# A two-layer decoder trunk: the down projection's seven-product scheme in two chunks of three groups instead of three of two, its sums read from PSUM by VectorE, and the SWA layer's norm factor and vector applied in one instruction

## The chip, the cores and the metric

One core of one Trainium2 chip. The metric is the device time of one execution in microseconds (us). Engines are named as the profile names them: PE (TensorE matmul), PEld (its weight loads), DVE (VectorE), ACT (ScalarE), POOL (GpSimd), SP (SyncE). A name such as L942 is line 942 of the kernel before.

## The reference, cut to what matters

512 tokens of width 1024 pass through two layers, a gated linear attention layer and a sliding-window attention (SWA) layer, each followed by a dense MLP of width 4096. Every sub-layer is wrapped in two norms:

```python
def rms_norm(x, w):
    y = x * lax.rsqrt(jnp.mean(x * x, axis=-1, keepdims=True) + NORM_EPS)
    return y * w

def sq_relu_mlp(h, w_up, w_down):
    return jnp.square(jax.nn.relu(h @ w_up)) @ w_down

for i in range(2):
    x = x + rms_norm(mixer(rms_norm(x, ln_mix_pre[i])), ln_mix_post[i])
    x = x + rms_norm(sq_relu_mlp(rms_norm(x, ln_mlp_pre[i]), w_up[i], w_down[i]), ln_mlp_post[i])
```

All is float32. The kernel multiplies in float32r with each operand split into a high part (a cast, on ACT) and a low part (source minus high, on DVE); a product takes three matmuls: high by high, high by low, low by high.

## The kernel before

The change touches two places: the MLP's down projection (`down`, run once in each of the two layers) and the norm ahead of the SWA layer (`prenorm`, run for four token tiles at the end of the first layer's down projection).

**Down projection.** The hidden activations (4096 wide) form 16 pairs of 256 rows, in eight groups g of two pairs; a group has four blocks a11, a12, a21, a22 (pair p by token half q). The first six groups (`SEVEN = 6`) are multiplied in the manner of Strassen: seven products of combined blocks instead of eight. They are taken in chunks of two groups, three chunks in a layer, each a call of `seven`. A call has seven phases, in the order 1, 2, 5, 3, 6, 7, 4. A phase does for each group of the chunk:

- `parts`: splits the group's weights v[g][p] (128x1024) into high and low, one ACT cast and one DVE subtraction through the helper lines L85 and L86, into two of the ten buffers of the pool "w";
- then starts the transfer that makes v[g][p] the next phase's combination: an accumulating DMA on POOL's queue (L947, `add`) that adds another block of weights from DRAM, or once a plain load on SP's queue (L951);
- `unit`: splits the activation block (128x512 in all) the same way into a slot of the pool "s" (25 slots);
- and then the matmuls: for token tile t = 0, all groups; for t = 1, all groups; six matmuls of 512 columns to each (L910 to L912). So a phase of two groups has 24.

After phase 2, four DVE instructions to each group (L955 to L958) combine the blocks in place and into `r5`.

Products 1, 5, 3 and 6 use the two PSUM banks of the tag "mm" in turn and are taken out by `collect`. Product 3 goes on adding in the banks of product 5; product 6 starts afresh in the same two banks. So phase 3 waits until `collect(5)` has read a bank, and phase 6 until `collect(3)` has. Products 2, 7 and 4 stay in PSUM (tags tp, ob, sc) over all chunks. `collect` does this: in the first chunk, two ACT copies into `sums[m]` (L942); in the later ones, two ACT copies into a slot `part` (L942) and one accumulating DMA on POOL's queue that adds it to `sums[m]` in SBUF (L944); for product 6 of the last chunk two DVE additions that read PSUM (L938).

Then DVE joins sums and banks (L972 to L976, and L980 and L982 for the banks B and E, which go on as the accumulators of the first output half), and groups 6 and 7 are added by plain products. In group 6 each weight pair (n, p) is loaded, split and multiplied with the four token tiles in the order t = 0 to 3; the first two tiles add to B (tag tp), the other two to E (tag sc).

**Norm ahead of the SWA layer.** For token tile t, `prenorm` squares x on ACT, multiplies x by the norm's vector on DVE into `xw` (L231), computes the factor r by five small POOL instructions, scales `xw` by r on ACT (L237), transposes it on PE (L240) and splits the result. The scaling is put by hand behind a count of products on PE (`later(4 * t + SCALE, ...)`, ordered by `tick`), and so are the transposes.

**Order.** The order of instructions on each engine is fixed when the program is built: earlier lines have priority, an instruction that by the builder's own costs isn't ready lets later ones pass, and buffers of a pool are given out as they come free. On the chip each engine then runs its list in order, so an instruction that waits holds back everything behind it on its engine.

Of the kernel before, what the change touches and what calls it, by code (L numbers as in the profile page):

```python
# [8 lines left out]
F32 = mybir.dt.float32  # L9
F32R = mybir.dt.float32r  # L10
U32 = mybir.dt.uint32
AF = mybir.ActivationFunctionType
ALU = mybir.AluOpType

P = 128
D = 1024
T = 512
NT = T // P
# [10 lines left out]
SEVEN = 6  # L29
# [6 lines left out]
ADD, SCALE, TURN, TURN_UP = 7, 11, 9, 7  # L36
# [4 lines left out]
def trunk(ctx: ExitStack, tc: tile.TileContext, x, vecs, g_qk, g_vg, g_lr, g_up, g_out,  # L41
          s_qkv, s_sinks, s_out, m_up, m_down, consts, out):
    nc = tc.nc
    act, dve, pe, pool = nc.scalar, nc.vector, nc.tensor, nc.gpsimd

    const = ctx.enter_context(tc.tile_pool(name="const", bufs=1))
    rawp = ctx.enter_context(tc.tile_pool(name="rawp", bufs=4))
# [11 lines left out]
    def name(s):  # L59
        nm[0] += 1  # L60
        return f"{s}_{nm[0]}"

    def slot(shape, dt=F32, n="s"):
        return sp.tile(shape, dt, tag="s", name=name(n))
# [102 lines left out]
    def later(when, insts):  # L167

        if ticks[0] is not None:
            plan.setdefault(when, []).extend(insts)  # L170
# [44 lines left out]
    def prenorm(t, wpre, hT):  # L215
        xt = x_t[t]
        xw = slot([P, D], n=f"xw{t}")
        if isinstance(hT, Blocks):
            for q in range(2):
                part = slice(q * 512, (q + 1) * 512)  # L220
                dve.tensor_mul(xw[:, part], xt[:, part], wpre[:, part])
                tb = tbank([P, 4, P])
                for k in range(4):
                    later(4 * t + TURN_UP, [pe.transpose(tb[:, k, :], xw[:, q * 512 + k * P:q * 512 + (k + 1) * P], ident)])
                hT.put(t, q, tb)
            return
        ss, v0 = small(2), small(1)
        for i in range(2):
            part = slice(i * 512, (i + 1) * 512)
            act.activation(junk, xt[:, part], AF.Square, accum_out=ss[:, i:i + 1])  # L230
            dve.tensor_mul(xw[:, part], xt[:, part], wpre[:, part])  # L231
        pool.tensor_scalar(v0, ss[:, 0:1], 1.0 / D, EPS, ALU.mult, ALU.add)
        r = rsqrt(ss[:, 1:2], 1.0 / D, base=v0)
        cols = slice(t * P, (t + 1) * P)
        for q in range(2):
            part = slice(q * 512, (q + 1) * 512)
            later(4 * t + SCALE, [act.activation(xw[:, part], xw[:, part], AF.Copy, scale=r)])  # L237
            tb = tbank([P, 4, P])
            for k in range(4):
                later(4 * t + TURN, [pe.transpose(tb[:, k, :], xw[:, q * 512 + k * P:q * 512 + (k + 1) * P], ident)])  # L240
            for kk in range(2):
                h, l = hT[2 * q + kk]
                split(h[:, :, cols], l[:, :, cols], tb[:, 2 * kk:2 * kk + 2, :])
# [643 lines left out]
    def down(layer, blk, post, done):  # L887
# [26 lines left out]
        sums = {m: slot([P, 2, 512], n=f"sum{m}") for m in (1, 5, 3, 6)}  # L914
        B, C, E = [tbank() for _ in range(2)], [bank(tag="ob") for _ in range(2)], [sbank() for _ in range(2)]

        def seven(gs, first, last):
            v, r5 = {}, {}
            for g in gs:
                v[g] = [rawp.tile([P, 1024], F32, tag="raw", name=name("raw")) for _ in range(2)]  # L920
                for p in range(2):
                    nc.sync.dma_start(v[g][p], source(g, p, 0))

            def phase(m, p, act_blk, acc, start, stop, after=None, cont=False):
                w, u = {}, {}
                for g in gs:
                    w[g] = parts(v[g][p])
                    if after:
                        after(g)
                    u[g] = unit(act_blk(g))  # L930
                for t in range(2):
                    for g in gs:
                        product(acc[t], u[g], w[g], t, start and g == gs[0], stop and g == gs[-1], cont)

            def collect(m, acc, direct=False):
                if direct:
                    for t in range(2):
                        dve.tensor_add(sums[m][:, t], sums[m][:, t], acc[t])  # L938
                    return
                to = sums[m] if first else slot([P, 2, 512], n=f"part{m}")  # L940
                for t in range(2):
                    act.copy(to[:, t], acc[t])  # L942
                if not first:
                    pool.dma_start(sums[m], to, accum_op=ALU.add)  # L944

            def add(p, q, n):
                return lambda g: pool.dma_start(v[g][p], source(g, q, n), accum_op=ALU.add)  # L947
            A = [bank() for _ in range(2)]
            phase(1, 0, lambda g: blk(g, 0, 0), A, True, True, add(0, 0, 1))
            collect(1, A)  # L950
            phase(2, 1, lambda g: blk(g, 1, 0), B, first, last, lambda g: nc.sync.dma_start(v[g][1], source(g, 1, 1)))  # L951
            for g in gs:
                a11, a12, a21, a22 = blk(g, 0, 0), blk(g, 1, 0), blk(g, 0, 1), blk(g, 1, 1)
                x = r5[g] = slot([P, 2, 256], n=f"r5{g}")
                dve.tensor_sub(x, a22, a21)  # L955
                dve.tensor_sub(a21, a11, a21)
                dve.scalar_tensor_tensor(out=a11, in0=x, scalar=-1.0, in1=a11, op0=ALU.mult, op1=ALU.subtract)
                dve.scalar_tensor_tensor(out=a12, in0=a11, scalar=-1.0, in1=a12, op0=ALU.mult, op1=ALU.subtract)  # L958
            A = [bank() for _ in range(2)]
            phase(5, 0, lambda g: r5[g], A, True, True, add(0, 1, 1))  # L960
            collect(5, A)
            phase(3, 1, lambda g: blk(g, 1, 0), A, False, True, add(1, 0, 1), True)
            collect(3, A)
            A = [bank() for _ in range(2)]
            phase(6, 0, lambda g: blk(g, 0, 0), A, True, True, add(0, 1, 0))
            collect(6, A, last)
            phase(7, 1, lambda g: blk(g, 0, 1), C, first, last)
            phase(4, 0, lambda g: blk(g, 1, 1), E, first, last)

        for c in range(0, SEVEN, 2):  # L970
            seven((c, c + 1), c == 0, c + 2 == SEVEN)
        dve.tensor_add(sums[6], sums[1], sums[6])  # L972
        dve.tensor_add(sums[3], sums[3], sums[6])
        for t in range(2):
# [3 lines left out]
        acc = [B + E, N]  # L978
# [12 lines left out]
        G = NF // 4  # L991
        for g in range(SEVEN, G):
            u, w = {}, {}
            for n in range(2):
                for p in range(2):
                    w[p, n] = load(g, p, n)
                    if n == 0:
                        for q in range(2):
                            u[p, q] = unit(blk(g, p, q))
                    if g < G - 1:  # L1000
                        for t in range(NT):
                            product(acc[n][t], u[p, t // 2], w[p, n], t % 2, False, False, True)
        ticks[0] = 0
        for t in range(NT):
            for n in range(2):
# [14 lines left out]
    first, raws, xws, rs, tbs, last = [], {}, {}, {}, {}, {}  # L1020
# [20 lines left out]
    for step in START.split():  # L1041
# [21 lines left out]
        if what == "q" and n == 0:  # L1063
# [3 lines left out]
            v = small(1)  # L1067
# [126 lines left out]
```

## Time and profile before

| | |
|---|---|
| median of 3 runs | 1087.16 us (1084.81 to 1090.80) |
| the profiled execution | 1085.77 us, of which span 1084.0 us |
| mean granted TensorE clock | 0.988 of full speed |
| busy: PE / DVE / ACT / POOL | 1047.5 / 772.3 / 679.5 / 179.3 us |
| first layer's down projection | about 400 to 572 us |
| second layer's down projection | about 904 to 1076 us |

A row of a timeline gives start, duration, engine, line, operation, and in square brackets the idle time ahead of the instruction and what ended it. Matmuls overlap in the pipeline: their durations are longer than the distance between their starts, and the distance is what counts. A row of the lines' view has busy time and mean duration, then idle time ahead and its releasers.

### The profile page before, as it was taken

Reading aid. Unit: us, or ns where it says so; the run is one execution under the profiler, and the core shown is the slowest. Engines: PE = TensorE matmul, PEld = TensorE weight load, DVE = VectorE, ACT = ScalarE, POOL = GpSimd, SP = SyncE. Lnnn points to the kernel's source line nnn. Section 1 sums busy time; section 2 is a strip of 40 time slices with the busy share of each in tenths; the row PEclk is TensorE's granted clock in tenths of the full one; section 3 lists DMA queues with packets and bytes.
Section 4 is the critical chain, followed back from the end, with each engine's and each line's share of the span. In section 5 each row is a group of like instructions: output and inputs, shape, how many; then the busy total and the mean of one; then the engine's idle time right before and its main releaser. Section 6 shows DMA issues by size and latency. Waiting matters only on the chain. (4 is left out here: it accounts for less than half of the span.)

```text
span 1084.0 us, 16766 instructions
## 1 busy us (share of the span) xinstructions
PE 1047.5 (97%) x6236; PEld 920.0 (85%) x6236; DVE 772.3 (71%) x1281; ACT 679.5 (63%) x1374; POOL 179.3 (17%) x345
## 2 busy tenths in 40 slices
PE   8999999999999999999998999999999999899997
PEld 5888888899999997877787899889999998677775
DVE  5666538588776867758746789779877777676764
ACT  7774436377676786556445688647766777665632
POOL 2001110256000011212025001027300001121202
PEclk9999999999999999999998999999999999999998
DMA  7323122232233267898714542012333336889922
GB/s 274 136 63 113 59 78 80 76 98 79 80 116 115 81 166 184 173 229 190 210 53 136 163 111 79 25 54 79 118 97 98 104 109 148 200 181 231 214 79 78
DMA packets 39220, 134.35 MB, mean 124 GB/s; under 512 B 4705, under 2 KB 4833, under 8 KB 39138
## 3 DMA queue, kind: packets, MB, share of 16 engines
q1 hardware_dynamic: 30210, 100.76, 29.1%
q0 software_dynamic: 8928, 32.51, 16.1%
q8 instruction: 49, 0.80, 0.3%
q14 instruction: 33, 0.27, 0.1%
HBM read 119.62 MB, written 2.10 MB: 112 GB/s over the span
## 5 line engine op out<-in xcount | busy, mean ns | idle before, releaser
L86 DVE TENSOR_TENSOR w<-raw,w 128x1024 fp32r<-128x1024 f32 x184 | 208.6, 1141 | 129.1 <-ACT w L85 127.2
L85 ACT CAST w<-raw 128x1024 fp32r<-128x1024 f32 x184 | 180.3, 982 | 129.6 <-DMA raw<-in_m_down_dram 53.4
L947 POOL DMA_DIRECT2D raw<-in_m_down_dram x48 | 42.3, 881 | 401.1 <-DVE a L855 261.2
L910 PE MATMUL mm<-w,u 128*128 128x512 f32 x224 | 90.6, 404 | 9.5 <-ACT part L942 5.3
L836 PE MATMUL A<-Sh,w 128*128 128x256 f32 x336 | 95.5, 284 | 0.0
L838 PE MATMUL A<-Sh,w 128*128 128x256 f32 x336 | 95.0, 283 | 0.0
L837 PE MATMUL A<-Sl,w 128*128 128x256 f32 x336 | 95.0, 283 | 0.0
L912 PE MATMUL mm<-w,u 128*128 128x512 f32 x224 | 89.6, 400 | 1.5 <-DVE u L86 0.9
L911 PE MATMUL mm<-w,u 128*128 128x512 f32 x224 | 88.8, 397 | 0.0
L85 ACT CAST wh<-raw 128x512 fp32r<-128x512 f32 x92 | 54.2, 621 | 30.8 <-PE ob L157 12.5
L86 DVE TENSOR_TENSOR wl<-raw,wh 128x512 fp32r<-128x512 f32 x92 | 60.3, 684 | 17.4 <-ACT wh L85 15.4
L836 PEld LDWEIGHTS A<-Sh,w 128*128 128x128 f32 x336 | 64.3, 191 | 1.2 <-ACT a L848 1.2
L837 PEld LDWEIGHTS A<-Sl,w 128*128 128x128 f32 x336 | 64.4, 192 | 0.0
L838 PEld LDWEIGHTS A<-Sh,w 128*128 128x128 f32 x336 | 64.4, 192 | 0.0
L910 PEld LDWEIGHTS mm<-w,u 128*128 128x128 f32 x224 | 43.0, 192 | 21.9 <-ACT part L942 6.6
L86 DVE TENSOR_TENSOR u<-a,u 128x512 fp32r<-128x512 f32 x88 | 57.0, 684 | 4.7 <-ACT u L85 4.7
L912 PEld LDWEIGHTS mm<-w,u 128*128 128x128 f32 x224 | 43.0, 192 | 13.5 <-DVE u L86 4.5
L911 PEld LDWEIGHTS mm<-w,u 128*128 128x128 f32 x224 | 43.2, 193 | 8.7
L85 ACT CAST u<-a 128x512 fp32r<-128x512 f32 x88 | 50.0, 621 | 0.0
L786 ACT ACTIVATE a<-a 128x256 f32<-128x256 f32 (+1 forms) x96 | 45.9, 491 | 1.3
L85 ACT CAST w<-tt 128x1024 fp32r<-128x1024 f32 x28 | 29.4, 1050 | 13.6 <-PE C L837 7.1
L86 DVE TENSOR_TENSOR w<-tt,w 128x1024 fp32r<-128x1024 f32 x28 | 34.2, 1222 | 2.3 <-ACT w L85 2.2
(387 smaller groups left out, 3306.3 us busy)
## 6 DMA issues: line engine op xcount, KB each, us to landing
raw<-in_m_up_dram SPq DMA_DIRECT2D x64, 512.0 KB, 3.6
raw<-in_m_down_dram SPq DMA_DIRECT2D x52, 512.0 KB, 5.8
raw<-in_m_down_dram POOLq DMA_DIRECT2D x48, 512.0 KB, 7.3
raw<-in_g_vg_dram SPq DMA_DIRECT2D x16, 512.0 KB, 4.1
sum<-part POOLq DMA_DIRECT2D x14, 512.0 KB, 8.9
raw<-in_s_qkv_dram SPq DMA_DIRECT2D x10, 512.0 KB, 3.6
raw<-in_g_qk_dram SPq DMA_DIRECT2D x8, 512.0 KB, 3.6
raw<-in_g_out_dram SPq DMA_DIRECT2D x8, 512.0 KB, 3.6
```

Source lines behind the costliest of these rows:

```text
L85: act.copy(h, src)
L86: dve.tensor_sub(l, src, f(h))
L786: act.activation(v, v, AF.Square)
L836: pe.matmul(acc, lhsT=wh[:, kc], rhs=h[:, k], start=first, stop=False, skip_group_check=not fresh)
L837: pe.matmul(acc, lhsT=wh[:, kc], rhs=l[:, k], start=False, stop=False, skip_group_check=not fresh)
L838: pe.matmul(acc, lhsT=wl[:, kc], rhs=h[:, k], start=False, stop=last, skip_group_check=not fresh)
L910: pe.matmul(acc, lhsT=ah[:, j, tc_], rhs=wh[:, wc], start=first and j == 0, stop=False, **kw)
L911: pe.matmul(acc, lhsT=ah[:, j, tc_], rhs=wl[:, wc], start=False, stop=False, **kw)
L912: newest[0] = pe.matmul(acc, lhsT=al[:, j, tc_], rhs=wh[:, wc], start=False, stop=last and j == 1, **kw)
L947: return lambda g: pool.dma_start(v[g][p], source(g, q, n), accum_op=ALU.add)
```

## The change

Chunks of three groups, so two calls of `seven` to a layer; a phase then has 36 matmuls. The weights of the third group have no buffer in the pool of raw weights and take two slots of the pool "s". `collect` copies with ACT in the first chunk as before, and in the second adds on DVE from PSUM: no `part`, no accumulating DMA for the sums. In group 6 both weight pairs of an output half are split first, and then all products of token tiles 0 and 1 run ahead of those of 2 and 3. In `prenorm` the multiplication by the vector (DVE) and the scaling by r (ACT) become one DVE instruction, where the scaling stood.

```diff
 prenorm:
             act.activation(junk, xt[:, part], AF.Square, accum_out=ss[:, i:i + 1])
-            dve.tensor_mul(xw[:, part], xt[:, part], wpre[:, part])
 ...
-            later(4 * t + SCALE, [act.activation(xw[:, part], xw[:, part], AF.Copy, scale=r)])
+            later(4 * t + SCALE, [dve.scalar_tensor_tensor(out=xw[:, part], in0=xt[:, part], scalar=r, in1=wpre[:, part], op0=ALU.mult, op1=ALU.mult)])
 seven:
-                v[g] = [rawp.tile([P, 1024], F32, tag="raw", name=name("raw")) for _ in range(2)]
+                v[g] = [rawp.tile([P, 1024], F32, tag="raw", name=name("raw")) if g < gs[2] else slot([P, 1024], n="raw") for _ in range(2)]
 ...
-            def collect(m, acc, direct=False):
-                if direct:
-                    for t in range(2):
+            def collect(m, acc):
+                for t in range(2):
+                    if first:
+                        act.copy(sums[m][:, t], acc[t])
+                    else:
                         dve.tensor_add(sums[m][:, t], sums[m][:, t], acc[t])
-                    return
-                to = sums[m] if first else slot([P, 2, 512], n=f"part{m}")
-                for t in range(2):
-                    act.copy(to[:, t], acc[t])
-                if not first:
-                    pool.dma_start(sums[m], to, accum_op=ALU.add)
 ...
-            collect(6, A, last)
+            collect(6, A)
 ...
-        for c in range(0, SEVEN, 2):
-            seven((c, c + 1), c == 0, c + 2 == SEVEN)
+        for c in range(0, SEVEN, 3):
+            seven((c, c + 1, c + 2), c == 0, c + 3 == SEVEN)
 groups 6 and 7:
-                    if g < G - 1:
-                        for t in range(NT):
-                            product(acc[n][t], u[p, t // 2], w[p, n], t % 2, False, False, True)
+                if g < G - 1:
+                    for q in range(2):
+                        for p in range(2):
+                            for t in range(2):
+                                product(acc[n][2 * q + t], u[p, q], w[p, n], t, False, False, True)
```

## Rows read from the trace of the kernel before

**Rows 1.** Part 1 of the page: busy time, share of the span and instructions of each engine.

```profile
PE 1047.5 (97%) x6236; PEld 920.0 (85%) x6236; DVE 772.3 (71%) x1281; ACT 679.5 (63%) x1374; POOL 179.3 (17%) x345
```

**Rows 2.** What PE waited for, over the whole span: us in total, times, longest.

```profile
PE mm L910 <- ACT part L942: 5.3, 3, 2.5
PE mm L910 <- ACT sum L942: 4.0, 2, 2.8
PE sc L156 <- ACT wh L85: 3.0, 1, 3.0
PE sc L910 <- DVE sc L982: 2.4, 2, 1.4
```

**Rows 3.** PE's timeline: the first layer's fourth matmul of phase 1 (399.89), the first and last of phases 7 and 4 of the first chunk (428.70 and 439.35, the 48th), and the first on bank E of group 6 (529.40); then the same two points of the second layer.

```profile
399.89 0.40 PE L910 MATMUL mm<-w,u 128*128 128x512 f32 x1
...
428.70 0.39 PE L910 MATMUL ob<-w,u 128*128 128x512 f32 x1
...
439.35 0.39 PE L912 MATMUL sc<-w,u 128*128 128x512 f32 x1
...
529.40 0.50 PE L910 MATMUL sc<-w,u 128*128 128x512 f32 x1 [1.44 <-DVE sc L982]
...
904.38 0.40 PE L910 MATMUL mm<-w,u 128*128 128x512 f32 x1
...
1035.07 0.50 PE L910 MATMUL sc<-w,u 128*128 128x512 f32 x1 [1.00 <-DVE sc L982]
```

**Rows 4.** Five stretches that start behind a wait of PE: length, busy time and instructions of PE, PEld, DVE, ACT and POOL, granted TensorE clock, DMA share, GB/s. The first four lie in the two down projections, the last where the SWA layer begins.

```profile
467.30:470.60 3.30, 3.30 (x8) 2.62 (x9) 2.62 (x4) 1.99 (x4) 0.90 (x1) 0.50 1.07 268
491.20:494.40 3.20, 3.20 (x10) 2.43 (x9) 3.20 (x6) 2.72 (x5) 0.89 (x1) 0.50 0.99 177
931.60:934.80 3.20, 2.79 (x7) 2.23 (x8) 2.93 (x4) 2.65 (x6) 0.00 (x0) 0.50 0.92 315
976.00:979.20 3.20, 3.20 (x9) 2.43 (x9) 1.37 (x3) 0.48 (x1) 0.00 (x0) 0.50 1.03 287
583.40:590.00 6.60, 5.37 (x23) 5.08 (x24) 4.76 (x9) 3.55 (x7) 5.46 (x17) 0.50 0.68 223
```

**Rows 5.** PE's timeline in phase 6 of the first layer's first chunk: the first matmul of its second token tile.

```profile
425.84 0.50 PE L910 MATMUL mm<-w,u 128*128 128x512 f32 x1 [1.22 <-ACT sum L942]
```

**Rows 6.** ACT's timeline around the same moment, and at the start of the first layer's third chunk.

```profile
421.55 1.05 ACT L85 CAST w<-raw 128x1024 fp32r<-128x1024 f32 x1
424.25 1.04 ACT L85 CAST w<-raw 128x1024 fp32r<-128x1024 f32 x1 [1.65 <-DMA raw<-in_m_down_dram]
425.20 1.07 ACT L942 COPY sum<-mm 128x512 f32<-128x512 f32 x2
...
483.45 1.05 ACT L85 CAST w<-raw 128x1024 fp32r<-128x1024 f32 x1 [3.97 <-DMA raw<-in_m_down_dram]
```

**Rows 7.** POOL's timeline: the issue of the accumulating transfer of the first group's weights in phase 6 of the first chunk.

```profile
416.60 0.87 POOL L947 DMA_DIRECT2D raw<-in_m_down_dram  x1 [1.96 <-DMA raw<-in_m_down_dram]
```

**Rows 8.** DMA of the first layer's down projection (395 to 560 us): the queue that POOL fills (packets, MB, share of 16 engines' time), then the two kinds of its transfers (count, KB each, median us from issue to landing); last, the issue of the sums' transfers in the lines' view of the whole span.

```profile
q0 software_dynamic: 4464, 16.25, 52.7%
...
raw<-in_m_down_dram POOLq DMA_DIRECT2D x23, 512.0 KB, 7.5
...
sum<-part POOLq DMA_DIRECT2D x7, 512.0 KB, 9.2
...
L944 POOL DMA_DIRECT2D sum<-part x14 | 12.3, 879 | 45.0 <-ACT part L942 32.8 <-issue 9.8 <-ACT u L85 2.4
```

**Rows 9.** The first layer's three chunks, one row to each; columns as in rows 4.

```profile
399.90:439.50 39.60, 38.25 (x167) 30.69 (x166) 30.39 (x38) 26.91 (x39) 7.01 (x8) 1.00 0.80 185
439.50:482.30 42.80, 40.14 (x169) 32.27 (x168) 29.82 (x36) 24.55 (x35) 10.58 (x12) 0.96 0.91 204
482.30:521.00 38.70, 36.95 (x154) 29.30 (x152) 28.15 (x37) 22.88 (x34) 7.95 (x9) 0.96 0.93 212
```

**Rows 10.** DVE's timeline at the end of the combination of blocks in the first chunk, and the subtractions behind it (the one at 409.32 belongs to the cast of rows 11, first line).

```profile
408.12 0.68 DVE L86 TENSOR_TENSOR u<-r,u 128x512 fp32r<-128x512 f32 x1
408.72 0.68 DVE L958 SCALAR_TENSOR_TENSOR a<-a,a 128x512 f32<-128x512 f32 x1
409.32 1.22 DVE L86 TENSOR_TENSOR w<-raw,w 128x1024 fp32r<-128x1024 f32 x1
...
411.06 3.49 DVE L86 TENSOR_TENSOR w<-raw,w 128x1024 fp32r<-128x1024 f32 x3
```

**Rows 11.** ACT's timeline in the first chunk: two casts of weights; the second waits for PE to be done with a buffer.

```profile
403.68 1.06 ACT L85 CAST w<-raw 128x1024 fp32r<-128x1024 f32 x1
...
408.73 1.06 ACT L85 CAST w<-raw 128x1024 fp32r<-128x1024 f32 x1 [1.28 <-PE tp L911]
```

**Rows 12.** The instructions on the tile `sum`: the DVE additions that read PSUM (durations in ns, minimum, median, maximum; first and last start).

```profile
L938 DVE TENSOR_TENSOR sum<-sum,mm x4: 680/680/681, 513.6 to 1022.0; 128x512 f32<-128x512 f32 x4
```

**Rows 13.** SP's timeline: the four loads of weights with which the first chunk begins (start of the first issue, time to the end of the last).

```profile
379.27 12.08 SPq L922 DMA_DIRECT2D raw<-in_m_down_dram  x4
```

**Rows 14.** The norm ahead of the SWA layer: the instructions on the tile `xw` (columns as in rows 12), and the DVE form with a factor and two tensors, from the lines' view.

```profile
L231 DVE TENSOR_TENSOR xw<-x,bc x8: 680/682/686, 558.5 to 583.5; 128x512 f32<-128x512 f32 x8
L237 ACT ACTIVATE xw<-xw,st x8: 706/722/753, 561.6 to 586.5; 128x512 f32<-128x512 f32 x8
...
L288 DVE SCALAR_TENSOR_TENSOR x<-fw,st,x 128x512 f32<-128x512 f32 x32 | 22.6, 747 | 13.9 <-POOL st L138 13.9
```

## The prediction

> **What bounds the kernel now.** I read the page's busy shares first: PE is busy 97% of the span [rows 1], so a gain must come out of the gaps and slow stretches of PE, and no other engine's total matters by itself. Next, what PE waited for: the longest entries are the matmuls of the down projection behind the ACT copies of `collect`, 5.3 + 4.0 = 9.3 us in five waits, then 2.4 us behind the DVE addition to bank E, and one wait of 3.0 us where the SWA layer starts [rows 2].
>
> The waits table shows only idle time, so I measured the stage from PE's timeline. Undisturbed, 48 matmuls start within 439.35 - 428.70 = 10.65 us, that is 0.2266 us from start to start [rows 3]. From the fourth matmul of the stage to the first on bank E in group 6 there are 504 + 12 + 1 - 4 = 513 such steps (seven products, six groups, two token tiles, six matmuls; then 12 of group 6), 116.2 us of work. The trace has 129.5 us for it in the first layer and 130.7 us in the second [rows 3]. So **13.3 + 14.4 = 27.7 us are lost** in the two down projections ahead of that point, 2.5% of the time. Of these 9.3 us are the waits on `collect`, 2.4 us those on E. Four stretches of 3.2 to 3.3 us behind such waits ran at a granted clock of 0.50 (1.2 GHz), each half lost: 6.5 us [rows 4]. The other 9.5 us are many waits below a microsecond.
>
> **Why PE waits for a copy of half a microsecond.** In phase 6 of the first chunk PE stands before the second token tile until 425.84 [rows 5]. ACT made that copy only at 425.20, because a cast of weights stood ahead of it in its list and waited for a DMA until 424.25 [rows 6]. That cast belongs to phase 4, two phases further on; its weights were being added to by a transfer that POOL had issued at 416.60 [rows 7], 7.6 us earlier, and 7.5 us is the median of these [rows 8]. So the chain is: accumulating transfer, cast far ahead, copy held behind it, PE. The same delay shows at the third chunk's start, where a cast waits 3.97 us for its load [rows 6].
>
> **Part 1: three groups to a phase.** Matmuls, casts and subtractions stay the same in number. A phase gets 36 x 0.2266 = 8.16 us in place of 5.44 us. Phases that must wait for a `collect` (3 and 6) number 8 in place of 12 in both layers. A bank finished at a phase's middle or end has 18 x 0.2266 = 4.08 us until it is needed again, not 2.72 us: by itself this takes 1.36 us off each of the long waits (1.2 to 2.8 us). More weighs that ten buffers hold five split weight pairs: with two groups that is two and a half phases ahead, with three one and two thirds. A cast needs the buffers of the pair five places back. The cast that held the copy (first of phase 4) now needs a pair of phase 6 to be finished, so it can't stand ahead of the copies of product 3. Casts that can (first two of phase 7) read weights whose transfers would be issued some 14 us earlier (an estimate: a phase and a half of 8.16 us and the 1.7 us until a buffer is free), nearly twice the 7.5 us of rows 8.
>
> **Part 2: sums on DVE.** Seven accumulating transfers of 512 KB go in each layer. POOL's queue took 52.7% of 165 us, 87 us of all 16 engines, for 23 + 7 transfers: 2.9 us each [rows 8], so about 20 us of DMA time are freed in a stage whose DMA share is 0.80 to 0.93 [rows 9]. POOL's list loses 14 issues that waited 32.8 us for copies, with later weight transfers queued behind them [rows 8]. ACT loses 14 copies in each layer; DVE gains 6 additions of 0.68 us [rows 12]. DVE's wait for a bank holds the subtractions behind it, as ACT's did, but with the longer lead above.
>
> Of the 25.3 us lost other than on E, I take three quarters as gone: **-19 us** (bounds 0 and -25.3; near the upper, since cast and transfer, the links that row after row shows, are both moved).
>
> **Part 3: the heavier burst on DVE.** The combination behind phase 2 grows from 8 to 12 instructions at 0.60 us from start to start [rows 10], 7.2 us in place of 4.8. In the second chunk DVE has 21 weights x 1.16 + 21 activations x 0.60 + 12 x 0.60 + 8 additions x 0.60 = 49 us in 57.1 us of PE, 86%; it was busy 28 to 30 us in chunks of 39 to 43 us before [rows 9, 10]. The old burst cost PE nothing, as no long wait of rows 2 stands there. New price between 0 and, if 2.4 us more in each of four chunks come through with 1.6 us of low clock each, 16 us. I take **+2.5 us**, near the rows of before.
>
> **Part 4: start of the stage.** SP loads four weights first, a series of 12.08 us, 3.0 us apart [rows 13]; the third group's come fifth and sixth, in two "s" slots that the up projection's operands must leave. The fifth would be issued at about 394.4, some 4 us later be there, and split by about 400.7; its matmuls are due at about 402. Cover 1 us: a cost of 0 to 3.0 us (one more step of that series) in each layer; **+1.5 us** in all.
>
> **Part 5: bank E.** Group 6 now runs 24 matmuls on B ahead of E, not 12: 2.7 us more than the waits of 1.44 and 1.00 us [rows 3]. What DVE does up to that addition only loses its waits for transfers. **-2.4 us** (0 to -2.4). The second weight pair is due 2.7 us earlier; its load is ready by then, as the loads queue behind fewer transfers.
>
> **Part 6: the norm step.** Off ACT go 8 x 0.72 us, off DVE 8 x 0.68, onto DVE 8 x 0.75 [rows 14]; behind r stand two DVE instructions instead of two ACT ones, +0.1 us a tile. PE's 3.0 us there wait for a cast on ACT [rows 2], followed by 6.6 us at half clock [rows 4]: with ACT freer it may go altogether (-6.3 us), or the new step may hold DVE's weight subtractions and double it (+3.0). The cast's place in ACT's list isn't changed by the edit itself: **-1 us**.
>
> **Sum.** -19 + 2.5 + 1.5 - 2.4 - 1 = -18.4 us on the profiled execution's 1085.8, that is 1067.4. That execution lies 1.4 us below the median of 1087.16; against the median it is **1068 us**.
>
> **Rivals.** (a) *DVE becomes the bound* in the burst: two to four chunks pay 2.4 + 1.6 us in place of my 2.5 in all, 1074 to 1082, say 1078. For it: 86% busy, work moved to the busier engine (DVE 71%, ACT 63% [rows 1]); a subtraction was already held 4.6 us by the burst (cast ended at 404.74, subtraction at 409.32 [rows 10, 11]). Against it: the burst's inputs are there early. The Trainium skill, Perfetto Trace Analysis, section Optimizing Scalar/DVE Operations, speaks for it: where DVE is saturated, work may better go to ScalarE, and here it goes the other way. By that rule alone (a) would hold; rows 9 show no saturated DVE. Chance 0.17.
>
> (b) *The transfers stay late*, whatever leaves the queue: the weights' own transfers remain 24 of 30 in each layer, the list order puts casts ahead of collecting again, and parts 1 and 2 give nothing. Then parts 5 and 6 alone remain: 1084, no change. For it: the first chunk had no sums' transfers and stalled all the same [rows 5, 6]. Chance 0.13.
>
> (c) *Slower: the third weight pair of each phase comes late.* Its buffers come free when the first pair of the phase before is done, 2.72 us ahead of the phase; it is due 2.72 us into the phase; cast and subtraction take 1.05 + 1.22 us. Cover: 3.1 us. Casts do wait for buffers today (1.28 us [rows 11]). If lists on ACT and DVE hold it by more, each microsecond counts in 28 phases: at the 4.6 us shown above 1.5 x 28 = 42 us, less the 21.4 us of parts 1, 2 and 5: 1108. It turns the sign from 3.9 us on. Against it: 4.6 us was one case, behind the burst. Chance 0.10.
>
> **Numbers.** Forecast 0.60, (a) 0.17, (b) 0.13, (c) 0.10. A measurement of this kernel tells about 0.5%, 5.4 us, from no change. Faster: forecast and (a), 0.77; same: (b), 0.13; slower: (c), 0.10. The range goes from 1053 (all of 27.7 us and 6.3 us gone) to 1084 (b) and leaves out (c).
>
> **What would show it.** Right: PE's waits on L942's copies fall from 9.3 us to under 2, on L982 to nothing; no stretch at clock 0.50 within the stage, at most one; 513 steps take under 122 us in each layer; ACT's casts wait for DMA far less than before; DMA share in the stage under 0.85. For (a): waits of PE on DVE's u or w in phase 5. For (b): L942 or L938 in PE's waits as long as before. For (c): waits one third into every phase on w. Wrong altogether would be a new wait outside the two places, from buffers of "s" that the third group's weights now hold.

## The result, and the profile after

| | before | after |
|---|---|---|
| median, both run on the same chip | 1087.09 us (4 runs, 1084.81 to 1090.80) | 1055.53 us (4 runs, 1055.18 to 1056.62) |
| ratio, 95% interval | | 0.9708 [0.9680, 0.9736] |
| profiled execution | 1085.77 us, span 1084.0 | 1056.62 us, span 1054.9 |

The change gives 31.6 us, 2.9%; the forecast was 19 us (1068 us). The kernel before scatters by some 10 us and four runs of it are few: the same two kernels once more, with eleven runs of the one before (after_again below), give 27.1 us, 0.9750 [0.9734, 0.9766]. The two profiled executions differ by 29.1 us of span, and these I account for.

Part 1 of the page, answering to [rows 1]: DVE has gained 6 us of work and ACT has lost 20 us. PE's busy time falls by 12 us with the same 6236 instructions, partly since fewer of them ran at the low clock.

```profile
PE 1035.5 (98%) x6236; PEld 917.3 (87%) x6236; DVE 778.6 (74%) x1293; ACT 659.7 (63%) x1338; POOL 170.0 (16%) x331
```

What PE waited for, over the whole span, answering to [rows 2]. No line of the down projection is in it; the two waits of the first row are the new norm step's.

```profile
PE tp L239 <- DVE xw L236: 3.2, 2, 1.7
PE tp L1086 <- ACT xw L1082: 1.8, 1, 1.8
PE tp L1050 <- DVE t L1011: 1.6, 1, 1.6
PE A L837 <- DVE w L86: 1.3, 8, 0.2
```

PE's timeline, answering to [rows 3]: fourth matmul of each down projection and first on bank E; between them the first matmul of the attention scores in the SWA layer (594.42).

```profile
400.81 0.40 PE L909 MATMUL mm<-w,u 128*128 128x512 f32 x1
...
520.00 0.39 PE L909 MATMUL sc<-w,u 128*128 128x512 f32 x1
...
594.42 0.44 PE L694 MATMUL sb<-kd,q 128*128 128x128 f32 x3
...
889.61 0.40 PE L909 MATMUL mm<-w,u 128*128 128x512 f32 x1
...
1008.82 0.39 PE L909 MATMUL sc<-w,u 128*128 128x512 f32 x1
```

Group 6 now runs 12 more matmuls ahead of E, so these are 525 steps, at 0.2266 us 119.0 us; the trace has 119.19 and 119.21. **Of 27.7 us lost before, 0.5 are left.** The scores begin 74.42 us behind E. Before they began at 609.15, 79.75 us behind E, or 77.03 without the 12 matmuls that now lie ahead of E: 2.6 us more saved. The stage begins 0.92 us later. From the scores to the second layer's fourth matmul both kernels take 295.2 us. Sum: -27.2 - 2.6 + 0.9 = -28.9 of the 29.1 us.

The stretches between those points (columns as in [rows 4]), then PE's only half-clock stretch in what the change touches; then, in either layer, a stretch from the last phase of the first chunk into the second in which DVE ran without a gap:

```profile
400.80:520.00 119.20, 119.20 (x527) 98.42 (x526) 105.87 (x133) 75.53 (x105) 18.48 (x21) 1.00 0.80 189
889.60:1008.80 119.20, 119.20 (x527) 98.41 (x526) 106.05 (x133) 75.53 (x105) 18.29 (x21) 1.00 0.79 187
...
578.60:582.00 3.40, 3.40 (x18) 3.40 (x18) 1.18 (x3) 0.67 (x3) 0.34 (x3) 0.51 0.81 246
...
450.00:494.00 44.00, 44.00 (x196) 36.45 (x195) 44.00 (x59) 29.95 (x43) 10.58 (x12) 1.00 0.90 183
...
938.80:982.80 44.00, 44.00 (x196) 36.44 (x195) 44.00 (x60) 29.72 (x43) 10.45 (x12) 1.00 0.89 178
```

The granted clock is 1.00 in both stages, where [rows 9] had 0.96 in two chunks of three. DMA share is 0.80 and 0.79. The last two rows are the surprise: DVE is busy for 44.00 of 44.00 us, and PE too. DVE has nothing to spare there and still delays nothing.

ACT's timeline around the phase of [rows 6]. Every copy of `collect` waits for PE alone, or for nothing: no cast that waits for a DMA stands ahead of one.

```profile
422.51 0.59 ACT L937 COPY sum<-mm 128x512 f32<-128x512 f32 x1 [1.71 <-PE mm L911]
422.99 1.66 ACT L85 CAST u<-a 128x512 fp32r<-128x512 f32 x3
425.00 0.59 ACT L937 COPY sum<-mm 128x512 f32<-128x512 f32 x1 [0.35 <-PE mm L911]
425.48 2.00 ACT L85 CAST w<-raw 128x1024 fp32r<-128x1024 f32 x2
429.08 0.59 ACT L937 COPY sum<-mm 128x512 f32<-128x512 f32 x1 [1.60 <-PE mm L911]
```

The weight casts in the lines' view of the whole span (busy, mean ns | idle time ahead, main releasers), first after, then before. The largest share of the idle time, 53.4 of 129.6 us, was spent on DMA; now the largest are PE's, that is, a buffer that PE still reads, as is to be expected of an engine that runs ahead.

```profile
L85 ACT CAST w<-raw 128x1024 fp32r<-128x1024 f32 x184 | 179.7, 982 | 114.0 <-PE mm L910 41.1 <-PE sc L910 23.1 <-PE B L836 19.1
```

```profile
L85 ACT CAST w<-raw 128x1024 fp32r<-128x1024 f32 x184 | 180.3, 982 | 129.6 <-DMA raw<-in_m_down_dram 53.4 <-PE B L837 21.0 <-PE sc L911 16.2
```

The part spent on DMA in after, from what ACT waited for over the whole span (us, times, longest):

```profile
ACT w L85 <- DMA raw<-in_m_down_dram: 2.8, 3, 1.7
```

DMA of the first layer's stage (395 to 548 us), answering to [rows 8]: 45.6% of 153 us for 24 transfers is 2.9 us each, as before. They land after 6.2 us instead of 7.5, and the seven of the sums are gone. Then the sums' additions on DVE, answering to [rows 12].

```profile
q0 software_dynamic: 3456, 12.58, 45.6%
...
raw<-in_m_down_dram POOLq DMA_DIRECT2D x24, 512.0 KB, 6.2
```

```profile
L939 DVE TENSOR_TENSOR sum<-sum,mm x16: 672/676/686, 462.7 to 987.3; 128x512 f32<-128x512 f32 x16
```

### The profile page after: what moved, and what is told of

Its sections match the earlier page's. It is cut to its first block, busy times and chain, and to the rows that moved or that the text cites. A ratio compares the mean times of both kernels' runs of the same rounds, so it can differ in the third digit from the quotient of the medians.

```text
span 1054.9 us, 16709 instructions
## 1 busy us (share of the span) xinstructions
PE 1035.5 (98%) x6236; PEld 917.3 (87%) x6236; DVE 778.6 (74%) x1293; ACT 659.7 (63%) x1338; POOL 170.0 (16%) x331
## 3 DMA queue, kind: packets, MB, share of 16 engines
q1 hardware_dynamic: 30210, 100.76, 29.2%
q0 software_dynamic: 6912, 25.17, 13.2%
## 5 line engine op out<-in xcount | busy, mean ns | idle before, releaser
L910 PE MATMUL mm<-w,u 128*128 128x512 f32 x224 | 87.5, 391 | 0.0
L909 PE MATMUL mm<-w,u 128*128 128x512 f32 x224 | 87.3, 390 | 0.0
L911 PE MATMUL mm<-w,u 128*128 128x512 f32 x224 | 87.3, 390 | 0.0
L86 DVE TENSOR_TENSOR wl<-raw,wh 128x512 fp32r<-128x512 f32 x92 | 60.5, 685 | 15.1 <-ACT wh L85 13.1
L911 PEld LDWEIGHTS mm<-w,u 128*128 128x128 f32 x224 | 42.0, 188 | 9.1
L910 PEld LDWEIGHTS mm<-w,u 128*128 128x128 f32 x224 | 42.1, 188 | 9.0 <-DVE w L86 0.5
L909 PEld LDWEIGHTS mm<-w,u 128*128 128x128 f32 x224 | 42.1, 188 | 8.3
L85 ACT CAST w<-tt 128x1024 fp32r<-128x1024 f32 x28 | 29.4, 1049 | 13.3 <-PE C L836 7.4
```

Of the source, the lines that this page charges most:

```text
L85: act.copy(h, src)
L86: dve.tensor_sub(l, src, f(h))
L909: pe.matmul(acc, lhsT=ah[:, j, tc_], rhs=wh[:, wc], start=first and j == 0, stop=False, **kw)
L910: pe.matmul(acc, lhsT=ah[:, j, tc_], rhs=wl[:, wc], start=False, stop=False, **kw)
L911: newest[0] = pe.matmul(acc, lhsT=al[:, j, tc_], rhs=wh[:, wc], start=False, stop=last and j == 1, **kw)
```

## The experiments

Theory 1 is the prediction's: late accumulating transfer, cast far ahead in ACT's list, copy of `collect` behind it, PE; more lead or fewer transfers cures it. Its rivals are named in each expectation. "Lost" is the time from the fourth matmul of the down projection to the first on E, over the undisturbed 0.2266 us a step (first layer + second); before, it is 13.3 + 14.4. The next column is the part of it up to the end of the first chunk, where no kernel has a sums' transfer. The last is how long ACT's weight casts waited for the weights' transfers, in the whole kernel.

| kernel | median us | ratio to before [95%] | lost us | in the first chunk | casts waited us |
|---|---|---|---|---|---|
| before | | | 13.3 + 14.4 | 2.3 + 5.3 | 53.4 |
| three_alone | 1072.03 | 0.9894 [0.9863, 0.9925] | 8.4 + 5.5 | 0.3 + 0.2 | 13.2 |
| sums_alone | 1066.27 | 0.9832 [0.9797, 0.9868] | 4.6 + 2.6 | 4.2 + 2.6 | 29.9 |
| six_alone | 1084.38 | 1.0007 [0.9986, 1.0027] | 12.4 + 17.0 | 2.8 + 7.2 | 56.9 |
| norm_alone | 1080.40 | 0.9974 [0.9955, 0.9993] | 10.2 + 12.8 | 2.4 + 2.2 | 52.0 |
| three_halves | 1064.60 | 0.9829 [0.9800, 0.9858] | 2.5 + 2.0 | 0.3 + 0.3 | 14.0 |
| copy_then_add | 1080.43 | 0.9971 [0.9947, 0.9995] | 9.8 + 15.1 | 2.3 + 6.9 | 43.2 |
| dve_copies | 1094.74 | 1.0108 [1.0069, 1.0146] | 15.6 + 18.0 | 3.4 + 2.2 | 69.3 |
| copies_first | 1079.12 | 0.9958 [0.9941, 0.9975] | 13.0 + 9.2 | 0.1 + 0.0 | 45.8 |
| after_again | 1055.08 | 0.9750 [0.9734, 0.9766] | 0.3 + 0.3 | 0.3 + 0.2 | 5.7 |
| after_old_six | 1056.44 | 0.9760 [0.9743, 0.9776] | 0.3 + 0.3 | 0.3 + 0.3 | 3.3 |
| norm_behind | 1056.23 | 0.9759 [0.9744, 0.9774] | 0.3 + 0.3 | 0.2 + 0.2 | 3.4 |
| after_eight | 1108.43, one run | | 1.0 + 1.0 | 1.0 + 1.0 | 2.8 |

The kernel before had medians of 1082.44, 1083.15 and 1082.92 us beside the first four, the next four and the last four; gains in us below are the ratio's share of these. "Lost" is read from one profile each and scatters by some us: norm_alone leaves the down projection as it was and shows 23.0 where before shows 27.7.

**three_alone**: the kernel before with chunks of three groups and nothing else.

```diff
-                v[g] = [rawp.tile(...) for _ in range(2)]
+                v[g] = [rawp.tile(...) if g < gs[2] else slot([P, 1024], n="raw") for _ in range(2)]
-        for c in range(0, SEVEN, 2):
-            seven((c, c + 1), c == 0, c + 2 == SEVEN)
+        for c in range(0, SEVEN, 3):
+            seven((c, c + 1, c + 2), c == 0, c + 3 == SEVEN)
```

> Before, with the chunks of three groups alone: sums still collected by ACT copies and, in the second chunk, added by transfers (4 in each layer instead of 7); group 6 and the norm as before. Theory 1 (the loss came from casts of weights that stood ahead of the copies of product 3 in ACT's list and waited for a transfer; phases of three groups with ten buffers take them out from there): nearly all of the 25 us outside bank E go, 1060 to 1066 us, PE waits on L942 under 1.5 us in total (9.3 before), the second chunk as clean as the first. Theory 2 (the transfers were late because the sums' transfers share the DMA engines and POOL's list): only the first chunk is clean, the second keeps waits of 2 us and more on L942 with stretches at half clock, 1070 to 1078 us. Bank E's 2.4 us stay in both.

Measured: 0.9894, 11.5 us: the time that theory 2 asked for, with the copies as theory 1 had them. The waits on the copies are gone in both chunks, the first included. (The sums' transfers left are three in each layer, not four as the expectation has it: product 6 of the last chunk was added by DVE before, too.) But in phase 4 of the second chunk PE stands, and runs at a granted clock of 0.52 from 513 to 520 us. PE's waits, then PE's, ACT's and POOL's timelines there:

```profile
PE sc L910 <- ACT w L85: 6.1, 2, 4.1
...
PE sc L911 <- DVE w L86: 1.8, 2, 1.0
```

```profile
513.83 0.80 PE L910 MATMUL sc<-w,u 128*128 128x512 f32 x1 [4.05 <-ACT w L85]
```

```profile
511.69 1.14 ACT L85 CAST u<-a 128x512 fp32r<-128x512 f32 x2 [5.34 <-DMA sum<-part]
512.73 1.04 ACT L85 CAST w<-raw 128x1024 fp32r<-128x1024 f32 x1
```

```profile
501.69 0.90 POOL L944 DMA_DIRECT2D sum<-part  x1 [4.20 <-issue]
```

The releaser of the activation cast looks absurd: a cast of `a` into `u` has nothing to do with `sum` and `part`. I read it as the slot: `u` takes over the "s" slot of a `part` that its transfer was still reading, and the weight cast that PE needs stands behind it. That the third group's raw weights had taken the spare slots is my reading of the program.

**sums_alone**: the kernel before with the sums of all chunks but the first added on DVE.

```diff
-                to = sums[m] if first else slot([P, 2, 512], n=f"part{m}")
...
-                    act.copy(to[:, t], acc[t])
-                if not first:
-                    pool.dma_start(sums[m], to, accum_op=ALU.add)
...
+                    if first:
+                        act.copy(sums[m][:, t], acc[t])
+                    else:
+                        dve.tensor_add(sums[m][:, t], sums[m][:, t], acc[t])
```

> Before, with the sums read by DVE alone: three chunks of two groups, no sums' transfers, all else as before. Theory 1: the casts of phase 4 still stand ahead of what takes product 3 out in the first chunk, so its 7 us stay in both layers together (4.0 us of waits on L942 and the half clock behind them); in the other chunks the additions sit in DVE's list behind subtractions that wait for the same casts, so half of the loss at most goes: 1074 to 1082 us. Theory 2: chunks 2 and 3 become clean, only the first keeps its 7 us: 1066 to 1070 us.

Measured: 0.9832, 18.2 us, the rival's figure. What is left of the waits lies in the first chunk, which had no sums' transfers anyway:

```profile
PE mm L910 <- ACT sum L938: 4.0, 2, 2.8
```

So sums_alone clears the second and third chunks (0.5 us lost there in both layers together, 17.3 before), where three_alone clears the copies' waits everywhere and makes a new one.

**six_alone** and **norm_alone**: the kernel before with group 6's order, and with the norm step, as the change's diff has them, and nothing else.

> Before, with group 6's products in the new order alone (all of token tiles 0 and 1 ahead of 2 and 3). Both theories: the waits of PE on L982 (1.44 and 1.00 us) go, 24 matmuls lie ahead of bank E and not 12: 1084 to 1085 us (-2.4 to -3). Rival: the second weight pair, now due 2.7 us earlier, is late and PE waits for it instead: 1087 us, no change.

> Before, with the norm's factor and vector in one DVE instruction alone. The traces of before and after differ by 2.6 us between bank E and the first attention scores. If that comes from the norm: 1084 to 1085 us, the wait of 3.0 us on a cast of weights and the half clock behind it shorter, new waits of PE on xw from DVE of 1.5 us twice. Rival: it came from the other parts, which shift the lists: no change, 1086 to 1088 us, or up to 3 us slower, since PE waits for DVE's xw.

Measured: six_alone is no different (1.0007). The waits on E are gone, and others are longer (PE on DVE's u 4.5 us in four waits). norm_alone is 2.8 us faster (0.9974). From E to the scores it takes 77.44 us where before took 79.75. Over all the profiles kept, and without the 12 matmuls that lie behind E in the old order, this stretch is 72.9 to 75.2 us in the six with the new norm step and 76.0 to 78.6 in the eight with the old one; so the step is what shortens it. The 3.0 us on the cast [rows 2] are gone, and PE now waits 3.3 us in three pieces for `xw`. After has the same (3.2 us above), and its half-clock stretch is 3.4 us long where [rows 4] had 6.6.

The four single effects sum to -11.5 - 18.2 + 0.8 - 2.8 = -31.7 us. That it is the 31.6 us of the first measurement is an accident: against the 27.1 us of after_again some 5 us are counted twice, what both of the first two remove in the later chunks and at E. The next four ask which link is needed.

**three_halves**: three_alone, with `part` as two half tiles from another pool, each with its own transfer of 256 KB. The sums' transfers stay, the "s" slots are free.

```diff
-                to = sums[m] if first else slot([P, 2, 512], n=f"part{m}")
+                to = [sums[m][:, t] if first else half([P, 512], n=f"part{m}") for t in range(2)]
-                    act.copy(to[:, t], acc[t])
-                if not first:
-                    pool.dma_start(sums[m], to, accum_op=ALU.add)
+                    act.copy(to[t], acc[t])
+                    if not first:
+                        pool.dma_start(sums[m][:, t], to[t], accum_op=ALU.add)
```

> As three_alone (chunks of three groups, sums still by transfers), but `part` lies in two half tiles of the pool t and not in a slot of the pool s, and each half has its own transfer of 256 KB (twice the issues, the same bytes). In three_alone PE's waits on L942 were gone in both chunks, but an activation cast in phase 4 of the second chunk waited 5.3 us for a sums' transfer, whose source slot it was to take over. Theory 1b (the sums' transfers hurt three groups only through the slots they hold): the wait in phase 4 goes, 20 us or more below before, 0.980 to 0.983 of it, as little is left to lose as 4 us for the stage in both layers. Theory 2 (they make the weights' transfers late): it stays near three_alone, 0.988 to 0.991 of before, with casts of phase 4 waiting for weights.

Measured: 0.9829, 18.5 us, lost 4.5 us. No cast waits for a sums' transfer any more, and the waits in phase 4 fall from 7.9 us to 3.4 (PE on DVE's w), so the slot was most of them (the halves also land sooner, 6.1 us against 8.1 in the first layer, which this run doesn't part from the slot). What is left is a sums' transfer again, by another way: a join of the sums stands in DVE's list until the last one has landed, and the weight subtraction that PE waits for stands behind it.

```profile
508.67 1.23 DVE L973 TENSOR_TENSOR sum<-sum,sum 128x1024 f32<-128x1024 f32 x1 [5.76 <-DMA sum<-part]
...
510.61 1.22 DVE L86 TENSOR_TENSOR w<-raw,w 128x1024 fp32r<-128x1024 f32 x1
```

So with the slots free, six of 14 sums' transfers and 28 of 44 copies may stay at a price of 4.5 us.

**copy_then_add** (two groups; ACT copies into `part`, DVE adds that to the sum, no transfer) and **dve_copies** (two groups; DVE copies into `part`, the transfer stays) each take one half of what sums_alone takes. All three add the same 28 instructions to DVE's list:

```diff
 copy_then_add:
-                if not first:
-                    pool.dma_start(sums[m], to, accum_op=ALU.add)
+                    if not first:
+                        dve.tensor_add(sums[m][:, t], sums[m][:, t], to[:, t])
 dve_copies:
-                    act.copy(to[:, t], acc[t])
+                    if first:
+                        act.copy(to[:, t], acc[t])
+                    else:
+                        dve.tensor_copy(to[:, t], acc[t])
```

> Before, three chunks of two groups, with the sums' transfers replaced by DVE additions from `part` in SBUF: ACT's copies keep their place in ACT's list. It parts what sums_alone joined. If the transfers' load was what delayed chunks 2 and 3: as sums_alone, 0.981 to 0.986 of before, waits of PE on L942 only in the first chunk (about 4 us). If it was the copies' place in ACT's list: waits on L942 stay 8 to 10 us, 0.995 to 1.000 of before.

> Before, three chunks of two groups, with DVE in place of ACT copying to `part` in chunks 2 and 3, and the sums' transfers kept. If the transfers' load counts: no gain, 0.996 to 1.004 of before, PE waits on DVE's copies in place of ACT's. If the place in ACT's list counts: most of sums_alone's gain, 0.983 to 0.988.

Measured: 0.9971 and 1.0108, so neither half gives what the two give together, and neither theory had both: copy_then_add has the time of the second and the short waits on copies of the first (4.9 us, 4.0 of them in the first chunk), dve_copies is slower than both asked. Without the transfers (first two lines), many waits of 0.6 to 0.9 us on u take the copies' place; with them and without ACT's copies, PE waits longer on u and w, and ACT's casts wait 69.3 us for DMA, 53.4 before (last line):

```profile
PE mm L912 <- DVE u L86: 3.6, 5, 0.7
PE mm L910 <- ACT u L85: 3.1, 4, 0.9
```

```profile
L85 ACT CAST w<-raw 128x1024 fp32r<-128x1024 f32 x184 | 180.0, 981 | 156.7 <-DMA raw<-in_m_down_dram 69.3 <-PE B L837 21.0 <-PE sc L911 17.2
```

**copies_first**: the kernel before, ACT's list alone changed. A phase's weight casts are put behind the copies of two phases earlier, so that no cast far ahead can stand before a copy.

```diff
...
-            split(h, l, v)
+            c = act.copy(h, v)
+            if after is not None:
+                behind([c], after)
+            dve.tensor_sub(l, v, f(h))
...
-                    w[g] = parts(v[g][p])
+                    w[g] = parts(v[g][p], taken.get(mine - 2))
...
+                    taken[nth[0] - 1] = act.copy(to[:, t], acc[t])
```

> Before, with one thing changed in ACT's list: the weights' casts of each phase stand behind the copies that take out the product two phases earlier, in all chunks; no instruction more or less. Theory 1 (a copy is held by a cast that waits for its transfer): PE's waits on L942 fall from 9.3 us to under 2 us, also in the first chunk, and 10 to 16 us go, 0.985 to 0.991 of before. Theory 2: casts and transfers are then late themselves, and PE waits for u and w instead: 0.996 to 1.004 of before.

Measured: 0.9958, where theory 1 asked for more. PE waits on no copy any more, in any chunk, so the link is real. In the first chunk, from which [rows 5] and [rows 7] come, it was the whole of the loss: 0.1 us is left of 7.6, and nothing else was changed. But 22.2 us are lost in all, about as many as norm_alone's 23.0, and all of them behind that chunk. PE's waits now stand in phase 4 of the later chunks, on the weights themselves:

```profile
PE sc L913 <- ACT w L896: 5.0, 4, 1.9
PE sc L914 <- DVE w L899: 3.9, 6, 0.8
```

There the copy held behind a cast was where lateness was paid, not where it came from.

**after_again**, **after_old_six** (the changed kernel with group 6 in the old order), **norm_behind** (its norm instruction put behind the next tile's evacuation in DVE's list) and **after_eight** (its split weights in eight buffers, not ten, throughout the kernel):

```diff
 norm_behind:
...
+                    if n == 1:
+                        behind(scales.pop(t - 1, []), e)
 after_eight:
-    wp = ctx.enter_context(tc.tile_pool(name="wp", bufs=10))
+    wp = ctx.enter_context(tc.tile_pool(name="wp", bufs=8))
```

> The changed kernel once more, beside the two variants of it below on the same chip: 0.968 to 0.974 of before, no wait of PE on sums, u or w in the down projection.

> The changed kernel with group 6's products in the order of before: bank E is due after 12 matmuls, not 24. If the new order is worth the 2.4 us of part 5 by itself: 2 to 3 us slower than after_again. If bank E was late only because the sums came by transfers (in three_halves and sums_alone PE waited 0.15 to 0.18 us for it, with the old order): within 0.7 us of after_again, which isn't to be told from it.

> The changed kernel with one thing moved in DVE's list: the norm's new instruction of a token tile stands behind the evacuation of the next tile, which it held up while it waited for r (evacuations of the last tile ready at 565 us ran at 568.4). If that wait costs the last tile's chain: PE's second wait on xw (1.7 us) falls below 0.7 us, 1 to 2 us faster than after_again. If the chain through POOL is what sets it: no change.

> The changed kernel with eight buffers for split weights in place of ten, in the whole kernel; only its down projections are read (525 steps from the fourth matmul to bank E, 119.0 us undisturbed, 119.2 after the change). The third pair's buffers then come free 1.36 us ahead of its phase and not 2.72, which leaves 1.7 us of cover beyond cast and subtraction. If rival (c)'s cover is real and was near to its end: 5 to 25 us lost in each projection, PE waiting for w one third or two thirds into the phases. If it had room: under 3 us lost in each.

Measured: after_again gives 27.1 us, at 0.975 just outside what was expected. after_old_six is 1.4 us above it, with intervals that overlap, and has no wait on E either: in the changed kernel the new order buys nothing that shows. norm_behind changes nothing; PE still waits 2.6 us for `xw`. In after DVE stands ready at that point and waits for POOL's small instructions:

```profile
567.05 1.42 DVE L236 SCALAR_TENSOR_TENSOR xw<-x,st,bc 128x512 f32<-128x512 f32 x2 [1.73 <-POOL st L138]
```

after_eight, in its one execution, loses 1.0 us in each stage, at one buffer pair less: the third weight pair had that much cover to spare. The rest of its 53 us is elsewhere; PE waits 29.2 us in the up projection, which I did not pursue:

```profile
PE C L835 <- DVE a L848: 29.2, 8, 3.9
```

## Why the prediction was right, and where its sizes were off

| term | predicted | measured |
|---|---|---|
| hand-offs in the stage | -19 (0 to -25.3) | -24.8 |
| burst on DVE | +2.5 (0 to +16) | 0 |
| start of the stage | +1.5 (0 to +6) | +0.9 here, +0.1 in after_again |
| bank E | -2.4 | -2.4 |
| norm | -1 (-6.3 to +3) | -2.6 |
| sum | -18.4 | -28.9 |

**Hand-offs.** Direction and place were right, the term too small. The step that failed is "I take three quarters of the 25.3 us as gone": 24.8 went. The prediction gives no reason for the quarter left out; it would have been right to leave it out if the small waits had causes of their own. Once the split weights are ready early, the small waits go with the long ones, and the low clock behind them too: the four stretches of [rows 4] in the stage, half of whose time was lost, have no successor.

**The chain** was right link by link, and in the first chunk it is the whole cause: copies_first moves nothing but the casts and takes the loss there from 7.6 us to 0.1; chunks of three groups take it to 0.5; the kernels that keep two groups and ACT's order lose 4.6 to 10.0 there. In the later chunks it is one way among others in which too little lead shows: take it away, and PE stands before the weights of phase 4 instead. What three groups give is lead, and ACT's casts show it: they wait 13.2 and 14.0 us for the weights' transfers in three_alone and three_halves, 53.4 before. Chunks of three also leave fewer sums' transfers (six of 14) and copies (28 of 44), but those alone don't do it: with two groups the casts still wait 43.2 us when all the sums' transfers are gone (copy_then_add) and 29.9 when the copies are, too (sums_alone). With two groups, it took the transfers and the copies together to clear the later chunks; one of them alone gave 3.1 us or cost 11.7. Whether the copies' time on ACT or the slots of `part` makes the small waits of copy_then_add stays open.

**Part 1 needs part 2**, which the prediction lacked. It named the danger as its last sentence on what would be wrong altogether, buffers of "s" that the third group's weights hold, but gave it no price and no link to part 2. three_alone prices it: 8.4 + 5.5 us. Reading the sums from PSUM frees those slots, and no join waits for a transfer any more. Part 2 alone in turn leaves the first chunk's 6.7 us.

**The burst**, rival (a). Its premise came true, more than I allowed. I had counted 62 instructions and 49 us for DVE in the second chunk's 57.1 us; the trace has 71 or 72 and 55.4 us, mostly since the joins of the sums start before the chunk ends. From the phase ahead of it on, DVE runs 44 us without a gap. Its price did not come: no PE wait in either stage. In [rows 10] a subtraction was held 4.6 us by the burst. Here the burst starts at 406.78, and from 409.12 nine of its twelve instructions run in one piece until the weight subtraction at 414.55, whose cast had ended at 408.48: it is held 6.1 us, and still nothing waits for it. The cast, in ACT's timeline, and the start and end of that piece, in DVE's:

```profile
407.43 1.05 ACT L85 CAST w<-raw 128x1024 fp32r<-128x1024 f32 x1
```

```profile
409.12 0.68 DVE L951 TENSOR_TENSOR a<-a,a 128x512 f32<-128x512 f32 x1
...
412.74 0.68 DVE L950 TENSOR_TENSOR r<-a,a 128x512 f32<-128x512 f32 x1
413.34 0.68 DVE L953 SCALAR_TENSOR_TENSOR a<-a,a 128x512 f32<-128x512 f32 x1
413.94 0.68 DVE L951 TENSOR_TENSOR a<-a 128x512 f32<-128x512 f32 x1
414.55 1.21 DVE L86 TENSOR_TENSOR w<-raw,w 128x1024 fp32r<-128x1024 f32 x1
```

So a full engine delayed nothing here, since its work fitted in PE's time and ran ahead of it. How much more DVE would bear there was not tried. The Trainium skill (Perfetto Trace Analysis, section Optimizing Scalar/DVE Operations) says that with DVE saturated, work may better go to ScalarE. Here DVE is saturated in these 44 us, work went to it from ScalarE and the DMA queue, and the time fell: the measurement goes against taking that advice from the busy share alone. It doesn't speak for such moves as such: dve_copies, which moved work from ScalarE to DVE and nothing else, was 1.1% slower.

**Bank E.** The amount was right, and of its two reasons one holds. The place of 12 matmuls isn't needed: the wait goes without the new order (after_old_six), and in sums_alone it is 0.15 us with the old one. The other is that DVE's work up to that addition loses its waits, and this is what counts: in the kernel before, the first join of the sums stood behind a weight subtraction that waited 3.10 us for its cast (2.75 in the second layer), more than E was late.

```profile
519.79 1.23 DVE L86 TENSOR_TENSOR w<-raw,w 128x1024 fp32r<-128x1024 f32 x1 [3.10 <-ACT w L85]
520.94 1.22 DVE L972 TENSOR_TENSOR sum<-sum,sum 128x1024 f32<-128x1024 f32 x1
```

**Start of the stage.** The 1.5 us that the prediction set aside don't show: the first layer's fourth matmul starts at 399.4 to 401.3 us in the seven profiles with two groups and at 399.7 to 401.2 in the six with three groups and ten buffers, so the 0.9 us are within the scatter.

**Norm.** -2.6 us, against -1. A wait of 3.0 us on ACT's cast became two of 1.47 and 1.70 us on DVE, apart from each other, and the half-clock stretch behind them is 3.4 us instead of 6.6. Half of those 3.2 us is 1.6 us; another microsecond of it I have not traced. In after_again that stretch has no half clock at all and is 1.5 us shorter, so one profile tells this term to a microsecond or two.

**Rivals (b) and (c).** (b) fell for the whole, but holds for single parts: copy_then_add and copies_first, which give no more lead, land within 0.5% of before (sums_alone, which gives none either, gains 1.7%). (c) is refuted: cover was not only enough, in after_eight's profile it survives the loss of a buffer pair.

Of the signs named ahead, all came: no wait on the copies or on E, clock 1.00 in the stages, 119.2 us for 525 steps (122 was allowed for 513), casts that wait 2.8 us for DMA instead of 53.4, DMA share 0.80.

## What to carry to other kernels

When a stage loses time in many small waits on different engines, ask how far ahead of their use operands are prepared; making the unit of work larger (more groups to a phase, with buffers for their operands) lengthened that lead here, and moving the one instruction on which the longest wait stood cured one chunk and only moved the wait in the others. A releaser that has nothing to do with the waiting instruction's data means a shared buffer slot: look up which tile held it. And the effects of single parts don't add up: two parts that gave 11.5 and 18 us shared some 5 of it, and one had a flaw that the other removed.

## What the runs showed of the hardware

An accumulating transfer of 512 KB took 2.9 us of all 16 engines' time in before and after alike. The plain loads on the other queue took about 1.5 us (in after 24.5% of 153 us for 25 loads). The 14 sums' transfers were therefore worth some 40 us of DMA time in the kernel (an estimate, at 2.9 us each), in place of which DVE does six additions more in each layer, 0.68 us each.

The kernel that loses time in small waits also scatters more: 1079.6 to 1089.5 us over the 17 runs of the kernel before beside copies_first, 1054.1 to 1057.4 over 17 runs of the changed kernel and the two variants that time the same, after_old_six and norm_behind. A sum made on one profiled execution of such a kernel carries that scatter.
